# Meta queries transposed with the third block, output projections in held order with dealt-out splits, residual rows behind their group's weights

## The chip, the cores and the metric

The kernel runs on one core of one Trainium2 chip. The metric is the device time of one execution in microseconds (us); smaller is better. A core has five engines with a queue each, which run their instructions in order and wait for one another at semaphores: TensorE (PE: matrix products, with PEld for its weight loads), VectorE (DVE), ScalarE (ACT), GpSimd (POOL), and SyncE (SP), which here issues every transfer between the chip's memory and on-chip SBUF. Products land in PSUM, in banks of 512 float32 columns.

## The reference

Two layers of a hybrid decoder on 1024 tokens with 16 learned meta tokens ahead of them, so 1040 rows of 1024 numbers, float32.

```python
def hybrid_layer(x, ...):
    h = rms_norm(x, norm_g)
    z = h @ w_in                       # 1024 -> 6408 columns
    aq, ak, av, ag, mq, mk, mv, mi, mf, mo, mgate = split(z)
    q, k = rope(rms_norm(aq)), rope(rms_norm(ak))
    ya = sliding_window_sink_attention(q, k, av, sink) * silu(ag)     # 16 heads of 64, window 128
    mq, mk = silu(causal_depthwise_conv(mq, mk))
    hm = rms_norm(mlstm_chunkwise(mq, mk, mv, log_i, log_f))          # 4 heads, chunks of 64
    ym = hm * sigmoid(mo) * silu(mgate)
    return x + concatenate([ya, ym]) @ w_out                          # 2048 -> 1024 columns

def reference(x, meta, ...):
    h = concatenate([meta, x])
    for l in range(2):
        h = hybrid_layer(h, ...)
    return h[:, 16:]
```

Every query sees its window of 128 keys and all meta keys. In layer 0 the meta rows have queries of their own; in layer 1 they need none, since their outputs are dropped.

## The kernel before

The 1040 rows are nine tiles: tile 0 with the 16 meta rows, tiles 1 to 8 with 128 rows each (`TT`). Along the rows there are also three chunks of 272, 384 and 384 (`CH`); tiles 0 to 4 lie in the first two chunks, tiles 5 to 8 in the second and third. Every float32 product is made of a high part (a copy in the fp32r format, on ACT) and a low part (the remainder, a subtraction on DVE or POOL) of both operands, with three matmuls: high by high, high by low, low by high. So nearly every operand of PE comes with a *split*: a copy and a subtraction. Split activations stand in `H`, split weights in `RING`, which has eight slots of one weight tile. A weight arrives in one of two `raw` buffers.

A layer runs the key and value projection, then attention by pairs of heads (`j` = 0 to 7, the next projections woven between), then the mLSTM, then the output projection. PE's order in attention and mLSTM is written out by hand: `pin` keeps instructions in program order while `in_order[0]` is true (set at L1000, cleared at L1069). Elsewhere a scheduler that models the engines decides, before the kernel is built, in which order the instructions stand in each queue.

Attention of a pair goes by blocks of 128 queries (block 0 are the 16 meta queries, in layer 0 alone), in steps: `s1` the scores into bank S (L628), and the softmax; `s2` the transposes of the probabilities; `s3` and `s4` the products with the values into bank O (L692, L704), of which there is one, and the copies out of it. The next pair's meta queries are transposed by PE at L583 in step `s3` of block 5 into spare columns of that block's O bank, and `s4` of the block splits them with `q_put` (copies L561 and L562 on ACT, subtractions L563 and L564 on DVE). The next pair's scores of block 0 need the split.

The output projection multiplies 16 tiles of `k` (14 of them stored before in `spool` in memory, two in SBUF) with `w_out`. It first loads and splits all 16 times three chunks of y: load L1100, copy L1104, subtraction L1109 on DVE or, for every third `k`, on POOL. Then come four groups: tiles 0 to 4 (1 to 4 in layer 1) and tiles 5 to 8, each for the left and right half of 512 columns. In a group, 16 weights are loaded (L172), copied (L174, ACT) and subtracted (L175, every third on DVE, the others on POOL), and each is multiplied for all tiles of the group (L1135); in the last group the last eight weights are held and gone through tile by tile. The group's banks come from `pj`, `pss` and `po` in turn, two of each. At the end of a tile its residual rows are loaded (L1154), added on DVE (L1157) and stored (L1161, or the output at L1159). In layer 0 the square of the sum (L1162, ACT, written into the result's bank) gives the next norm: with the right half done, the left half is loaded back (L1165) and `norm_tile` scales (L285, DVE), transposes (L288, PE, eight per tile) and splits (L291 ACT, L292 DVE) into `H`.

Of the kernel before, what the change touches and what calls it, by code (L numbers as in the profile page):

```python
# [18 lines left out]
L = N_META + SEQ  # L19
# [43 lines left out]
def build(ctx, tc, I, O):  # L63
# [103 lines left out]

    def wout(l, k, c0, i):
# [3 lines left out]
        sy.dma_start(raw, I["w_out"][l][k * 128:(k + 1) * 128, c0:c0 + 512])  # L172
# [101 lines left out]
    def norm_tile(t, xh, ssq_ap, gbc):  # L274
# [5 lines left out]
        for g in range(2):  # L280
            if gbc is None:
                ve.tensor_scalar(xh[g][:p, :], xh[g][:p, :], v[:p, 1:2], None, ALU.mult)
            for i in range(2 if gbc is not None else 0):
                xs = xh[g][:p, 256 * i:256 * i + 256]
                ve.scalar_tensor_tensor(xs, xs, v[:p, 1:2], gbc[2 * g + i][:p, 0:256], ALU.mult, ALU.mult)  # L285
            ps = bank("pt")
            for k in range(4):
                pin(pe.transpose(ps[:, k * p:(k + 1) * p], xh[g][:p, k * 128:(k + 1) * 128], ident[:p, :p]))  # L288
            src = ps[:, 0:4 * p].rearrange("p (k t) -> p k t", k=4)
            hi = H[:, 4 * g:4 * g + 4, t0:t0 + p]  # L290
            sc.activation(hi, src, AF.Copy)  # L291
            ve.tensor_tensor(H[:, 8 + 4 * g:12 + 4 * g, t0:t0 + p], src, hi, op=ALU.subtract)  # L292
            if t == 0:
                for i in range(3):
                    ve.tensor_copy(HM[:, 4 * g:4 * g + 4, 16 * i:16 * i + 16],
                                   H[:, 4 * (g + i // 2 * 2):4 * (g + i // 2 * 2) + 4, 0:16])
# [15 lines left out]
    def first_norm(t, xt, G):  # L312
# [9 lines left out]
        norm_tile(t, xg, st[:p, 0:2], None)  # L322
# [29 lines left out]

    for l in range(DEPTH):
# [98 lines left out]
        def kv_tasks():  # L452
# [161 lines left out]
        def att_tasks(j, st):  # L614
# [67 lines left out]
            def s3(b):  # L682
# [3 lines left out]
                if b == 5 and j < 7 and first_q == 0:  # L686
# [407 lines left out]
        for i, k in enumerate(order):  # L1094
            ylo[k] = unit(F32R)
            for c, (t0, n, _) in enumerate(CH):
                a = s0 if c == 0 else t0
                if k < 14:
                    y = p512(F32, t0 + n - a) if (i + c) % 2 else t384(t0 + n - a)
                    sy.dma_start(y, spool[k, :, a:t0 + n])  # L1100
                else:
                    y = ym[k - 14][:, a:t0 + n]
                hi = H[:, k, a:t0 + n]
                sc.activation(hi, y, AF.Copy)  # L1104
                if a == 0:
                    sc.activation(ylo[k][:, L:L + 32], y[:, 0:32], AF.Copy)
                    gp.tensor_tensor(ylo[k][:, L + 32:L + 48], y[:, 0:16], ylo[k][:, L:L + 16], op=ALU.subtract)
                eng = gp if i % 3 == 2 else ve
                eng.tensor_tensor(ylo[k][:, a:t0 + n], y, hi, op=ALU.subtract)  # L1109
# [4 lines left out]
        pools = ["pj", "pss", "po"]  # L1114
        nb = 0
        for grp in (range(first_q, 5), range(5, 9)):
            for hf in range(2):
                c0 = 512 * hf
                pss_t = {}
                for t in grp:  # L1120
                    pss_t[t] = bank(pools[nb % 3])
                    nb += 1
                def product(i, k, t, w):
                    t0, p = TT[t]
                    ps = pss_t[t]
                    wh, wl = w
                    if t == 0:
                        st = ylo[k][:, L:L + 48]
                        terms = ((st, wh), (st, wl))
                        p = 48  # L1130
                    else:
                        hi, lo = H[:, k, t0:t0 + p], ylo[k][:, t0:t0 + p]
                        terms = ((hi, wh), (hi, wl), (lo, wh))
                    for n, (a, b) in enumerate(terms):
                        pin(pe.matmul(ps[:p, :], a, b, start=(i + n == 0), stop=(i == 15 and n == len(terms) - 1)))  # L1135

                cut = 16 - 8 if hf == 1 and grp[-1] == 8 else 16
                for i, k in enumerate(order[:cut]):
                    w = wout(l, k, c0, i)
                    for t in grp:  # L1140
                        product(i, k, t, w)
                tail = [(i, order[i], wout(l, order[i], c0, i)) for i in range(cut, 16)]
                for t in grp:
                    for i, k, w in tail:
                        product(i, k, t, w)
# [41 lines left out]
```

## Time and profile before

| | |
|---|---|
| runs, median of 3 | 1997.38 us (1996.06 to 1997.59) |
| the profiled execution, whole | 1995.97 us |
| its span, first to last instruction | 1994.2 us |
| PE busy | 1916.2 us, 96% |
| DVE, ACT, POOL busy | 1099.9, 1062.6, 929.9 us |
| mean granted TensorE clock | 0.99 |

PE is the engine to watch: what it does not work for is lost, while the others wait for some of the time anyway. In a row of the timeline, the square bracket holds the idle time of the engine just before that instruction and the instruction whose end released it. A row with x4 stands for four instructions that ran on end. A stretch's clock is a share of TensorE's full speed. Names such as `RING`, `raw` and `pj` are those of the code, and a line number is that of the instruction.

### The profile page before, as it was taken

What the parts mean: (1) busy time and instruction counts of PE and PEld (TensorE: products, weight loads), DVE (VectorE), ACT (ScalarE), POOL (GpSimd) and SP (SyncE); (2) the same over time, 40 slices, a digit from 0 to 9 for tenths busy, and PEclk for the clock granted to TensorE, in tenths of its full rate; (3) what the DMA queues carried; (4) which work ended last, traced back from release to release, by engine and by line L of the source; (5) the groups of instructions that cost most, each with busy time, mean ns of one, the idle gap of its engine ahead of it and who ended that gap; (6) DMA issues with size and microseconds to landing.
All of it is one profiled execution on the core that took longest, in us unless ns stands there. A gap on an engine that the chain in (4) does not pass through costs nothing. (4 is left out here: it accounts for less than half of the span.)

```text
span 1994.2 us, 36168 instructions
## 1 busy us (share of the span) xinstructions
PE 1916.2 (96%) x12823; PEld 1806.1 (91%) x12823; DVE 1099.9 (55%) x2969; ACT 1062.6 (53%) x3133; POOL 929.9 (47%) x1116
## 2 busy tenths in 40 slices
PE   6999899999999999989999999999999999999899
PEld 6899899999999999867879999999999999997787
DVE  8767767666445364541435677776573636347111
ACT  5567767655454544642324678777364545446221
POOL 7544544335555454553335345444365453646331
PEclk9999999999999999999999999999999999999999
DMA  5111111111212122453541111112122221217443
GB/s 160 43 33 42 42 44 37 35 53 45 57 47 69 36 59 58 146 170 115 162 144 49 48 36 51 45 36 58 38 58 62 39 76 38 61 47 232 145 141 106
DMA packets 149796, 147.71 MB, mean 74 GB/s; under 512 B 14952, under 2 KB 122768, under 8 KB 149616
## 3 DMA queue, kind: packets, MB, share of 16 engines
q1 hardware_dynamic: 149616, 145.41, 25.1%
q8 instruction: 101, 1.65, 0.4%
q14 instruction: 79, 0.65, 0.1%
HBM read 122.01 MB, written 23.29 MB: 73 GB/s over the span
## 5 line engine op out<-in xcount | busy, mean ns | idle before, releaser
L183 PE MATMUL pj<-H,RING 128*128 128x384 f32 (+2 forms) x3456 | 578.4, 323 | 0.3 <-ACT t L838 0.3
L183 PEld LDWEIGHTS pj<-H,RING 128*128 128x128 f32 x3456 | 546.1, 189 | 2.9 <-issue 0.7
L160 POOL TENSOR_TENSOR RING<-raw,RING 128x512 fp32r<-128x512 f32 (+1 forms) x196 | 260.6, 1337 | 137.8 <-ACT RING L159 125.4
L222 PE MATMUL pj<-RING,H 128*128 128x256 f32 (+1 forms) x1920 | 270.0, 287 | 1.9 <-DVE w1k L190 1.9
L222 PEld LDWEIGHTS pj<-RING,H 128*128 128x128 f32 x1920 | 244.0, 190 | 2.3 <-DVE w1k L190 2.2
L222 PE MATMUL pj<-H,RING 128*128 128x384 f32 (+2 forms) x1152 | 217.7, 327 | 3.0 <-DVE u L564 3.0
L175 POOL TENSOR_TENSOR RING<-raw,RING 128x512 fp32r<-128x512 f32 x88 | 115.0, 1311 | 196.8 <-ACT RING L174 192.4
L183 PE MATMUL pj<-RING,H 128*128 128x256 f32 x1536 | 200.8, 285 | 2.6 <-DVE H L292 1.5
L183 PEld LDWEIGHTS pj<-RING,H 128*128 128x128 f32 x1536 | 189.0, 189 | 4.0 <-DVE H L292 1.7
L174 ACT ACTIVATE RING<-raw 128x512 fp32r<-128x512 f32 x128 | 80.7, 632 | 202.2 <-DMA raw<-in_w_out_dram 134.1
L222 PEld LDWEIGHTS pj<-H,RING 128*128 128x128 f32 x1152 | 180.7, 191 | 3.8 <-PE T L668 1.3
L159 ACT ACTIVATE RING<-raw 128x512 fp32r<-128x512 f32 (+1 forms) x196 | 122.9, 629 | 73.3 <-DMA raw<-in_w_in_dram 48.2
L713 POOL TENSOR_TENSOR u<-u,w1k 128x128 f32<-128x128 f32 (+1 forms) x136 | 63.4, 466 | 176.8 <-DVE w1k L709 169.4
L175 DVE TENSOR_TENSOR RING<-raw,RING 128x512 fp32r<-128x512 f32 x40 | 31.5, 788 | 194.0 <-ACT RING L174 194.0
L679 POOL TENSOR_SCALAR_AFFINE_SELECT p<-p 128x512 fp32r<-128x512 f32 x112 | 72.2, 645 | 133.7 <-DVE p L675 131.1
L649 ACT ACTIVATE t<-S,mx 128x145 f32<-128x145 f32 (+1 forms) x272 | 100.3, 373 | 62.6 <-DVE mx L646 54.5
L882 POOL TENSOR_TENSOR p<-u,p 128x258 fp32r<-128x258 f32 x64 | 46.7, 730 | 169.2 <-ACT p L881 169.1
L1135 PE MATMUL pj<-RING,H 128*128 128x512 f32 x352 | 112.9, 400 | 7.1 <-DVE p L1157 5.8
L1135 PE MATMUL pss<-RING,H 128*128 128x512 f32 x352 | 113.5, 402 | 1.3 <-ACT H L1104 1.3
L824 DVE SCALAR_TENSOR_TENSOR t<-u,cw,t 128x384 f32<-128x384 f32 (+1 forms) x144 | 109.1, 757 | 2.6
L628 PE MATMUL S<-u 128*128 128x272 f32 (+2 forms) x544 | 87.5, 280 | 19.3 <-DVE u L563 16.3
L654 ACT ACTIVATE t<-t,mx 128x144 f32<-128x144 f32 (+1 forms) x272 | 97.6, 406 | 13.6 <-DVE mx L651 13.1
(342 smaller groups left out, 3834.0 us busy)
## 6 DMA issues: line engine op xcount, KB each, us to landing
raw<-in_w_out_dram SPq DMA_DIRECT2D x128, 256.0 KB, 2.8
raw<-in_w_in_dram SPq DMA_DIRECT2D x100, 256.0 KB, 2.8
raw<-in_w_in_dram SPq DMA_DIRECT2D x192, 128.0 KB, 2.3
spool<-u SPq DMA_DIRECT2D x56, 192.0 KB, 1.9
p<-x SPq DMA_DIRECT2D x24, 256.0 KB, 4.4
t<-spool SPq DMA_DIRECT2D x28, 192.0 KB, 3.5
p<-spool SPq DMA_DIRECT2D x28, 192.0 KB, 3.6
u<-em SPq DMA_DIRECT2D x8, 576.0 KB, 6.9
```

What stands on the lines that cost most here:

```text
L159: sc.activation(hi, raw[:, :, 0:o], AF.Copy)
L160: eng.tensor_tensor(lo, raw[:, :, 0:o], hi, op=ALU.subtract)
L174: sc.activation(hi, raw, AF.Copy)
L175: (ve if i % 3 == 2 else gp).tensor_tensor(lo, raw, hi, op=ALU.subtract)
L183: pin(pe.matmul(out, a, b, start=(i == 0), stop=(i == n - 1)))
L222: pin(pe.matmul(out(), x, y, start=(k + i == 0), stop=(k == n - 1 and i == 2)))
L628: pin(pe.matmul(S[:p, h, o + 2 - 2 * h:o + 2 - 2 * h + kn], lq, Ks[i][:, k0:k0 + kn], start=(i == 0), stop=(i == 1)))
L649: sc.activation(P[:p, 145 * h:145 * h + 145], S[:p, h, 1 + 127 * h:146 + 127 * h], AF.Exp, bias=mx[:p, 0, h:h + 1], accum_out=mx[:p, 1, h: ...
L654: sc.activation(Pn, Pn, AF.Copy, scale=mx[:p, 2, h:h + 1])
L679: gp.affine_select(OW, HL, [[0, 4], [1, 128]], ALU.is_ge, 0.0, base=0, channel_multiplier=-1)
L824: ve.scalar_tensor_tensor(z, RAW[:, t0 + i:t0 + i + n], wcol(i), z, ALU.mult, ALU.add)
L1135: pin(pe.matmul(ps[:p, :], a, b, start=(i + n == 0), stop=(i == 15 and n == len(terms) - 1)))
```

## The change

Three things, in the words of the diff's own parts. First, the meta queries are transposed in step `s3` of block 3 rather than 5, and split in `s4` of the same block.

```diff
-                if b == 5 and j < 7 and first_q == 0:
+                if b == 3 and j < 7 and first_q == 0:
                     st["QM"] = O[:, 256:272]
                     q_meta_turn(j + 1, st["QM"])
```

PE, attention of the first pair in layer 0, before (L583 is the transpose, S_1077 x4 of 16x16 the scores of the meta queries, L222 the woven projection):

```order
L222 MATMUL pj<-H,RING 128x384 x6
L583 MATMUL O<-cst,w1k 128x16
L692 MATMUL O<-p_1473,u 128x256 x2
L704 MATMUL O<-ptm_107,VM 128x128 x2
L704 MATMUL O<-p_1478,u 128x256 x2
L206 MATMUL pj<-RING,HM 48x256 x16
L628 MATMUL S_1077<-u 16x16 x4
```

and now (L594 is the transpose; the scores stand 25 rows behind it, after the same 16 matmuls of 48x256, L208):

```order
L594 MATMUL O<-cst,w1k 128x16
L703 MATMUL O<-p_1333,u 128x256 x2
L224 MATMUL pj<-H,RING 128x384 x6
L715 MATMUL O<-ptm_107,VM 128x128 x2
L715 MATMUL O<-p_1338,u 128x256 x2
...
L703 MATMUL O<-p_1479,u 128x256 x2
L715 MATMUL O<-ptm_107,VM 128x128 x2
L715 MATMUL O<-p_1484,u 128x256 x2
L208 MATMUL pj<-RING,HM 48x256 x16
L639 MATMUL S_1077<-u 16x16 x4
```

The transpose moved two blocks ahead; the scores did not move.

Second, the output projection. The y splits become a function of one `k` and one chunk, and are dealt to the groups: chunks 0 and 1 to the first, each pair ahead of its weight, chunk 2 to the second. Banks go round two by two. The last three weights of a group (six in the fourth) are held and gone through tile by tile. PE's order is the program's from the second group on. Of the weights' subtractions, the first nine of a group are POOL's, and of the rest every second is DVE's. The square goes to a bank of the tag `pt`. Residual rows are issued behind the group's last weight:

```diff
-        (ve if i % 3 == 2 else gp).tensor_tensor(lo, raw, hi, op=ALU.subtract)
+        (ve if i > 8 and i % 2 else gp).tensor_tensor(lo, raw, hi, op=ALU.subtract)
...
-        pools = ["pj", "pss", "po"]
+        pools = ["pj", "pj", "pss", "pss", "po", "po"]
...
+            with tc.issue_after(w_load[0]):
+                sy.dma_start(xr[:p, :], src)
...
+            in_order[0] = g > 0
...
+            cut = 10 if g == 3 else 13
+            chunks = ((0, 1), (2,), (), ())[g]
+            for i in range(cut):
+                for c in chunks:
+                    y_split(i, c)
+                w = wout(l, order[i], c0, i)
                 for t in grp:
+                    product(pss_t[t], i, t, w)
+                if g == 2 and not last:
+                    if i > 2:
+                        turn()
+                    if i % 2 and i < 10:
+                        norm_again(i // 2)
...
+            for t in grp:
+                for i, w in tail:
+                    product(pss_t[t], i, t, w)
+                    if g == 3 and i == 12:
+                        turn(3)
+                if g == 3:
+                    turn(2)
+                result(pss_t[t], t, hf)
+        in_order[0] = False
+        carry[:] = turns
```

SP's queue at the end of layer 0's first group, before (L172 loads a weight, L1100 a chunk of y, L1154 residual rows, L1161 stores a sum):

```order
L172 DMA raw<-in_w_out_dram 128x512
L1100 DMA p_11131<-spool 128x384
L1154 DMA p_11437<-in_meta_dram 16x512
L172 DMA raw<-in_w_out_dram 128x512
L1154 DMA p_11443<-in_x_dram 128x512
L1154 DMA p_11448<-in_x_dram 128x512
L1154 DMA p_11453<-in_x_dram 128x512
L172 DMA raw<-in_w_out_dram 128x512 x11
L1161 DMA x_96<-p_11443 128x512
```

and now (L174, L1115, L1159, L1170 are the same four):

```order
L1115 DMA t<-spool 128x384 x3
L174 DMA raw<-in_w_out_dram 128x512 x2
L1115 DMA t<-spool 128x384 x3
L174 DMA raw<-in_w_out_dram 128x512 x2
L1159 DMA p_11341<-in_meta_dram 16x512
L1159 DMA p_11357<-in_x_dram 128x512
L1159 DMA p_11372<-in_x_dram 128x512
L1159 DMA p_11387<-in_x_dram 128x512
L174 DMA raw<-in_w_out_dram 128x512 x7
L1170 DMA x_96<-p_11341 16x512
```

The residual rows stand behind all sixteen weights of their group now, where before weights of the group came after them.

DVE's queue between the first and the second group of layer 1, before (L1109 is a y subtraction, L175 a weight's, L1157 the addition of the residual rows, which frees a bank):

```order
L1109 TENSOR_TENSOR u<-p_22731,H 128x256
L1109 TENSOR_TENSOR u<-p_22739,H 128x384
L175 TENSOR_TENSOR RING<-raw,RING 128x512 x2
L1157 TENSOR_TENSOR p_23003<-pj,p_23003 128x512
L1157 TENSOR_TENSOR p_23007<-pss,p_23007 128x512
L1157 TENSOR_TENSOR p_23011<-po,p_23011 128x512
L1157 TENSOR_TENSOR p_23015<-pj,p_23015 128x512
```

and now (L1124, L177, L1162):

```order
L177 TENSOR_TENSOR RING<-raw,RING 128x512
L1162 TENSOR_TENSOR p_22952<-pj,p_22952 128x512
L1162 TENSOR_TENSOR p_22965<-pj,p_22965 128x512
L1162 TENSOR_TENSOR p_22978<-pss,p_22978 128x512
L1124 TENSOR_TENSOR u<-p_23019,H 128x384
L1162 TENSOR_TENSOR p_22991<-pss,p_22991 128x512
```

Before, two subtractions of weights of the second group stood ahead of the adds; now none does, and y subtractions of chunk 2 stand among and behind them.

Third, the norm at the end of layer 0. `norm_tile` is cut into `norm_pre` (the scale factor and the scaling) and `norm_half` (four transposes and the split of one half). Tiles 0 to 4, whose sums are complete after the second group, are loaded back and normed in the third (`norm_again` after weights 1, 3, 5, 7 and 9, one half after each of the weights 3 to 12). Tiles 5 to 8 are normed in the fourth, a half at a time within the tail of a later tile, and the last three halves, in `carry`, between the tiles of layer 1's key and value projection:

```diff
                 ps = projN(wg, t, 256)
+                if l > 0 and t != 1 and carry:
+                    carry.pop(0)()
                 ve.tensor_copy(KR[:p, t, :], ps[:p, 0:128])
```

The number of matmuls and transposes is the same as before. For tiles 5 to 8 the left half is loaded back as two transfers of 256 columns; for tiles 0 to 4 both halves are loaded back.

## Rows read from the trace of the kernel before

**Rows 1.** The page: busy us, share of the span, instructions

```profile
PE 1916.2 (96%) x12823; PEld 1806.1 (91%) x12823; DVE 1099.9 (55%) x2969; ACT 1062.6 (53%) x3133; POOL 929.9 (47%) x1116
```

**Rows 2.** Waits: engine, line, waited for: us in total, times, longest

```profile
PE S L628 <- DVE u L563: 16.3, 8, 5.9
...
PE pj L1135 <- POOL RING L175: 2.3, 1, 2.3
...
PE po L1135 <- ACT RING L174: 1.8, 1, 1.8
...
PE po L1135 <- POOL RING L175: 1.3, 2, 0.7
```

**Rows 3.** Timeline of PE: start, us, operation, count, [idle before <-releaser]

```profile
103.70 0.40 PE L692 MATMUL O<-p,u 128*128 128x256 f32 x2
...
108.45 0.49 PE L692 MATMUL O<-p,u 128*128 128x256 f32 x2
...
119.50 0.23 PE L583 MATMUL O<-cst,w1k 16*128 16x16 f32 x1
...
123.42 0.49 PE L628 MATMUL S<-u 128*16 128x16 f32 x4 [0.93 <-DVE u L563]
...
239.42 0.23 PE L583 MATMUL O<-cst,w1k 16*128 16x16 f32 x1
...
248.27 0.50 PE L628 MATMUL S<-u 128*16 128x16 f32 x4 [5.90 <-DVE u L563]
...
1109.38 0.52 PE L628 MATMUL S<-u 128*128 128x272 f32 x2 [0.95 <-DVE u L563]
```

**Rows 4.** Timeline of ACT at the longest wait

```profile
246.74 0.63 ACT L159 ACTIVATE RING<-raw 128x512 fp32r<-128x512 f32 x1 [0.58 <-DMA raw<-in_w_in_dram]
```

**Rows 5.** Stretches: us, busy of PE PEld DVE ACT POOL, clock, DMA, GB/s

```profile
244.80:251.60 6.80, 3.25 (x17) 3.11 (x18) 3.24 (x12) 3.42 (x12) 6.63 (x7) 0.50 0.37 106
330.20:333.60 3.40, 3.40 (x17) 3.33 (x17) 2.12 (x5) 0.87 (x4) 3.40 (x3) 0.51 0.22 65
890.00:896.80 6.80, 5.11 (x11) 2.95 (x12) 3.85 (x6) 4.48 (x11) 2.54 (x2) 0.50 0.55 186
1047.00:1050.40 3.40, 3.33 (x16) 3.33 (x17) 3.10 (x7) 2.26 (x6) 1.40 (x2) 0.51 0.33 84
1855.90:1862.70 6.80, 5.14 (x12) 4.12 (x13) 3.08 (x5) 1.66 (x4) 2.55 (x2) 0.50 0.63 204
100.00:400.00 300.00, 282.51 (x2160) 274.61 (x2159) 211.65 (x639) 213.53 (x724) 129.28 (x180) 0.98 0.14 39
1100.00:1400.00 300.00, 291.33 (x2235) 286.84 (x2235) 214.06 (x616) 215.05 (x702) 130.78 (x171) 0.99 0.16 45
```

**Rows 6.** Timeline of SP's queue and ACT, layer 0's first output group

```profile
863.96 1.41 SPq L1154 DMA_DIRECT2D p<-in_x_dram  x3
...
866.01 0.63 ACT L174 ACTIVATE RING<-raw 128x512 fp32r<-128x512 f32 x1 [3.88 <-DMA raw<-in_w_out_dram]
```

**Rows 7.** Timeline of DVE and PE, last norm of layer 0

```profile
1042.66 3.75 DVE L285 SCALAR_TENSOR_TENSOR p<-p,nv,w1k 128x256 f32<-128x256 f32 x4 [0.73 <-POOL nv L279]
...
1047.07 1.97 PE L288 MATMUL pt<-cst,p 128*128 128x128 f32 x8 [2.00 <-DVE H L292]
```

**Rows 8.** Timeline of DVE and PE, layer 1's output projection

```profile
1836.43 1.50 DVE L175 TENSOR_TENSOR RING<-raw,RING 128x512 fp32r<-128x512 f32 x1
...
1856.21 0.69 DVE L175 TENSOR_TENSOR RING<-raw,RING 128x512 fp32r<-128x512 f32 x1 [8.16 <-ACT RING L174]
...
1857.56 1.22 PE L1135 MATMUL pj<-RING,H 128*128 128x512 f32 x2 [5.85 <-DVE p L1157]
```

**Rows 9.** By line: ns min/median/max, first and last start; us to landing

```profile
L175 POOL TENSOR_TENSOR RING<-raw,RING x88: 1257/1292/1734, 797.4 to 1969.1; 128x512 fp32r<-128x512 f32 x88
...
DMA to landing us min/median/max: 2.7/3.3/6.4
```

**Rows 10.** The chain that ended last: start, us, engine, tile, line, count

```profile
1870.14 1.39 PE pss L1135 x6
```

More of the change, by code (lines that the diff above doesn't have):

```diff
@@ L166, in wgroup @@
         return [(ps[k // 2][:, 0, k % 2], ps[k // 2][:, 1, k % 2]) for k in range(8)]
+    w_load = [None]
     def wout(l, k, c0, i):
@@ L321, in first_norm @@
             xg.append(y)
-        norm_tile(t, xg, st[:p, 0:2], None)
+        norm_pre(t, xg, st[:p, 0:2], None)
+        for g in range(2):
+            norm_half(t, g, xg[g:g + 1])
     snk = cp.tile([128, 2, HEADS], F32, name="snk")
@@ new lines, in build, with product @@
+        pools = ["pj", "pj", "pss", "pss", "po", "po"]
+        nb = [0]
+        turns = []
+        def product(ps, i, t, w):
+            k = order[i]
+            t0, p = TT[t]
+            wh, wl = w
+            if t == 0:
+                st = ylo[k][:, L:L + 48]
+                terms = ((st, wh), (st, wl))
+                p = 48
+            else:
+                hi, lo = H[:, k, t0:t0 + p], ylo[k][:, t0:t0 + p]
+                terms = ((hi, wh), (hi, wl), (lo, wh))
+            for n, (a, b) in enumerate(terms):
+                pin(pe.matmul(ps[:p, :], a, b, start=(i + n == 0), stop=(i == 15 and n == len(terms) - 1)))
@@ new lines, in result @@
+        def result(ps, t, hf):
+            t0, p = TT[t]
+            c0 = 512 * hf
+            xr = p512(F32)
+            if l > 0:
+                src = x1[t0:t0 + p, c0:c0 + 512]
+            elif t == 0:
+                src = I["meta"][:, c0:c0 + 512]
+            else:
+                src = I["x"][t0 - 16:t0 + 112, c0:c0 + 512]
+            with tc.issue_after(w_load[0]):
+                sy.dma_start(xr[:p, :], src)
+            if t == 0:
+                ve.tensor_tensor(xr[:16, :], ps[32:48, :], xr[:16, :], op=ALU.add)
+            ve.tensor_tensor(xr[:p, :], ps[:p, :], xr[:p, :], op=ALU.add)
+            if last:
+                sy.dma_start(O["out"][t0 - 16:t0 + 112, c0:c0 + 512], xr[:p, :])
+                return
+            if hf == 1 and t > 4:
+                x0 = [t384(256) for _ in range(2)]
+                for i, x in enumerate(x0):
+                    sy.dma_start(x[:p, :], x1[t0:t0 + p, 256 * i:256 * i + 256])
+            sy.dma_start(x1[t0:t0 + p, c0:c0 + 512], xr[:p, :])
+            sc.activation(bank("pt")[:p, :], xr[:p, :], AF.Square, accum_out=ssq[:p, t, hf:hf + 1])
+            if hf == 1 and t > 4:
+                norm_later(t, x0 + [xr[:, 0:256], xr[:, 256:512]])
@@ new lines, in norm_later, with norm_again, turn @@
+        def norm_later(t, xq):
+            norm_pre(t, xq, ssq[:TT[t][1], t, :], gbc)
+            turns.extend(lambda g=g: norm_half(t, g, xq[2 * g:2 * g + 2]) for g in range(2))
+        def norm_again(t):
+            t0, p = TT[t]
+            x = [p512(F32) for _ in range(2)]
+            for i in range(2):
+                sy.dma_start(x[i][:p, :], x1[t0:t0 + p, 512 * i:512 * i + 512])
+            norm_later(t, [y[:, o:o + 256] for y in x for o in (0, 256)])
+        def turn(least=1):
+            if len(turns) >= least:
+                turns.pop(0)()
```

133 lines of the change are left out of this document (49 added, 84 removed).

## The prediction

> **What bounds the kernel now.** I read the busy shares first: TensorE (PE) works for 96% of the span of 1994.2 us, the other engines for about half of it [rows 1]. 1994.2 − 1916.2 = 78.0 us of PE idle is thus all that a change which leaves the matmuls alone can win, with what TensorE loses while its clock is at the lower of its two levels. None of the edits takes matmuls out, so I looked for the idle stretches and their releasers, engine by engine: first the list of waits, then the timeline of PE at each wait, then the granted clock by stretches. Four places belong to lines that the diff touches.
>
> First, the attention of layer 0. The scores of the meta queries wait for a subtraction on VectorE (DVE) that makes their split: 16.3 us in eight waits [rows 2]. One of them, 0.95 us, is in layer 1 [rows 3], which has no meta queries, so 16.3 − 0.95 = 15.35 us in seven waits. The pattern is the first one: the transpose runs at 119.50, the scores at 123.42, that is 3.9 us later, 0.93 us of it idle. The worst has its transpose at 239.42 and its scores 8.85 us later, after 5.90 us of idle [rows 3]: there ScalarE's (ACT) queue held a weight split that waited for its own transfer [rows 4] ahead of the copy that frees the query.
>
> Second, the output projection of layer 0: 2.3, 1.8 and twice some 0.65 us (1.3 together) on weights that come late, 5.4 us [rows 2]. Just ahead of the first of them three residual rows are issued between the weights, and ACT then waits 3.88 us for a weight [rows 6]. Third, the last norm of layer 0: PE waits 2.00 us for the subtraction of a half that stands behind a scaling of 3.75 us on DVE [rows 7]. Fourth, the output projection of layer 1: 5.85 us at the start of the second group, for the adds that free the banks; DVE reached the add only when a weight subtraction ahead of it in its queue had run, after DVE had waited 8.16 us for that weight [rows 8].
>
> After most of these idles the granted clock is 0.50 for 3.4 or 6.8 us and 1.0 outside: the 1.2 GHz level instead of 2.4 [rows 5]. PE's work of such a stretch takes twice as long, so half of its busy time is lost: 3.25/2 = 1.6 us behind the wait at 248, 3.40/2 = 1.7 behind one at 329, 5.11/2 = 2.55 in layer 0's projection, 3.33/2 = 1.65 at the norm, 5.14/2 = 2.55 in layer 1's.
>
> **The change, part by part.**
>
> Meta queries two blocks earlier. It is the same number of instructions. The transpose (one instruction, 0.23 us) moves ahead of the third block's second matmuls, and the copies and subtractions on ACT and DVE follow it there, while the scores stay where they are, behind two more blocks of PE's work. Blocks follow one another by 108.45 − 103.70 = 4.75 us [rows 3], so the split has 9.5 us more, against a longest wait of 5.90. The wait goes: 15.35 + 1.6 + 1.7 = 18.7 us. It is not given for nothing: query columns lie in the O bank, of which there is one, and the next block's matmuls into it wait until the split has read them. That was so at the old place as well, with the same 3.9 us from transpose to split, under 4.75. If that cover is gone, the wait sits at the new place (a rival). What is late next are the waits that layer 1 has: its 300 us of attention hold 300 − 291.33 = 8.7 us of idle, layer 0's 300 − 282.51 = 17.5 [rows 5], of which 15.35 are ours, hence 2.1 of others. If layer 0 takes on layer 1's idle, 6.6 us come back; if not, none. The work on the other engines is alike, but layer 0's waits now cover up what layer 1's would show, so I take the middle, 3.3 us.
>
> Output projections of layer 0. The third chunk's 16 loads and splits leave the first group for the second, the residual loads go behind the group's last weight, and the nine first subtractions go to GpSimd (POOL). Groups take 16 weights; 12 matmuls a weight at 1.39/6 = 0.232 us [rows 10] are 2.8 us for a four-tile group, and 14 are 3.2 us with five tiles. A subtraction on POOL is 1.29 us [rows 9], so POOL keeps the pace. The four late weights come from loads queued behind other loads and from splits queued behind others, and both go: 5.4 + 2.55 = 7.9 us. Lower bound of this gain: if only the residual rows mattered, the first stall of 2.3; upper: 7.9, which I take, since weights now stand ahead of all that delayed them.
>
> The square goes to a bank of its own and six banks are dealt out in turn rather than three, so the second half of a group starts on free banks. It has no price of its own.
>
> Norm of layer 0 into the third group and the next layer's projection. The same transposes (eight a tile, nine tiles) are issued in halves between matmuls; PE pays for them as before. Nine reloads become ten of the same size and eight of half of it, on SP's queue behind weights. The last norm's wait is gone: 2.00 + 1.65 = 3.65 us. New waits: in the fourth group, the first half of tile 5 must be scaled within one tile's tail, 6 weights x 3 matmuls x 0.232 = 4.2 us, while the four scalings alone have taken up to 3.75 [rows 7]; and the turns in the next layer's projection stand on PE ahead of its tiles. I charge 0 to 2 us, and take 1.
>
> Layer 1. In the changed order the four adds stand ahead of any of the next group's subtractions on DVE, since its nine first weights are POOL's. The wait of 5.85 us and its lower clock go: 5.85 + 2.55 = 8.4 us. What is late next is the weight itself: the first group now holds three weights to its end and needs the last of them some 4 us earlier. The loads ahead of them on SP are fewer by 14 chunks, at 1.41/3 = 0.47 us of issue each [rows 6], so I take 0 and leave up to 3 us.
>
> Here a rule bears against the change. The rows show a weight's subtraction on DVE at 1.50 us in a stretch in which POOL subtracts too, where the same instruction takes 0.69 at another time [rows 8], and POOL's at up to 1.73 where 1.29 is the median [rows 9]. The Trainium skill, page "SBUF — State Buffer", section "Who interferes with whom", says that a DVE instruction with two SBUF inputs and a GpSimd instruction that reads SBUF exclude each other, one waiting until the other has ended; the rows agree. What the mechanism would cost here is rival E.
>
> **Sum.** 18.7 − 3.3 + 7.9 + 3.65 − 1 + 8.4 = 34.3 us. It is made against the profiled execution, 1995.97 us (span 1994.2 and 1.8 around it): 1961.6. The median of the runs, 1997.38, is 1.4 above that execution, so the forecast is 1963 us, 1.7% less.
>
> **The rivals.**
>
> A. The meta wait moves with the transpose: the O bank is held, and the next block's matmuls wait instead of the scores. For it: 3.9 us to the split against 4.75 between blocks leaves under 1 us, and the worst took 8.85. Against it: the bank was held in the same way at the old place, and no such wait is in the list for that line. It costs the 18.7 − 3.3 = 15.4 us: 1978.
>
> B. Supply of weights binds in the output projections: two raw buffers, held from the load's issue to the end of the subtraction, so that taking DVE's 0.69 out of the first nine puts weights late whatever the queue order. For it: ACT's wait of 3.88 [rows 6]. Against it: a load of that size lands in 2.7 to 3.3 us [rows 9], ACT's copy takes 0.63 [rows 6] and POOL 1.29, 4.6 to 5.2 together, over two buffers 2.3 to 2.6 a weight, and PE needs 2.8. Only attention and norm remain, 15.4 + 2.65 = 18.05 us: 1979.
>
> C. Slower. The reloads of the third group come late. There PE's order is fixed, ten half-tile turns stand between the products, and a reload that is late stops PE at each; the next weights stand behind it on SP. A row of that size lands in 3.3 us, at worst 6.4 [rows 9], and is scaled in up to 3.75 [rows 7]; from the turn that frees its buffers it has two steps of PE, 5.6 us. 3.3 + 3.75 − 5.6 = 1.5 us a turn are possible. From 34.3/10 = 3.4 us a turn on the whole gain is eaten; with the worst landing it is 6.4 + 3.75 − 5.6 = 4.6, and the ten cost 46 us: 1963 + 46 = 2009. Against it: the sums of squares of these tiles are complete a group earlier, and SP runs weights ahead of PE.
>
> D. It does not do what it says: new waits in the fixed order eat what goes, within 4 us (0.2%) of 1997, about what a measurement of this kernel can tell from no change.
>
> E. DVE and POOL hold each other up. Three more of each group's weights are POOL's, 3 x 1.29 = 3.9 us in which DVE's splits wait. In the first group of each layer PE needs those splits at once, so the two first groups lose 2 x 3.9 = 7.7 us: 1971. For it: the stretched subtractions above. Against it: POOL's 12 x 1.29 and DVE's 4 x 0.69 make 18.2 us even one after the other, in a group of 44 to 52, and a third of the splits leaves the first group.
>
> **How the numbers follow.** Forecast 0.67; A 0.10; B 0.09; C 0.04; D 0.04; E 0.06. The forecast's own range: low, where nothing comes back and no new wait appears (−4.3) and a further 1.7 us of a lower clock goes with the waits, 1957; I put 1955. High, 6.6 coming back, 2 of new waits, 3 in layer 1 and 2.3 instead of 7.9 in layer 0, +3.3 + 1 + 3 + 5.6: 1976. E lies inside; A and B end at 1979, which I take as the end. C and D lie outside. Faster 0.92, same 0.04, slower 0.04.
>
> **What would show it.** In the trace of after: the list of waits has no wait of the scores for the split above 1 us in total, and layer 0's 300 us of attention show PE at about 294 to 297 (right), or a wait of the second matmuls for VectorE's subtraction near 15 us (A). The projections show no idle above 1 us and no 0.50 clock at the starts of groups (right), or waits for the subtraction on GpSimd (B). In the third group of layer 0, a transpose that waits for a scaling or for a reload is C. The adds of layer 1 run within 1 us of their product's end (right). The forecast falls, in the good direction, if other idle of the 78 us goes as well; in the bad one, if the 0.50 clock appears in new places, as a stretch costs 1.7 to 2.6 us even where the idle before it is short.

## The result

The changed kernel takes 1969.84 us (median of 4 executions, 1967.16 to 1971.40) where the one before takes 1997.49 in the same comparison: a ratio of 0.9861 with a 95% interval of 0.9844 to 0.9878. That is 27.65 us less, where 34.3 were forecast; the time lies in the range, above the forecast of 1963. Its profiled execution took 1971.03 us, 24.9 below that of the kernel before.

The page of the changed kernel, first part (busy us, share of the span, instructions), against [rows 1]:

```profile
span 1969.3 us, 36180 instructions
...
PE 1906.4 (97%) x12823; PEld 1795.8 (91%) x12823; DVE 1099.3 (56%) x2961; ACT 1062.8 (54%) x3133; POOL 940.8 (48%) x1124
```

PE's idle time is now 1969.3 − 1906.4 = 62.9 us, 15.1 less. Its busy time is 9.8 us less for the same 12823 instructions, and it runs less of the time at the lower clock. By stretches of 2 us, the granted clock of before falls below 0.9 in nine places; after, two are left ahead of the last instructions, at 57 to 61 and at 409 to 413 us.

The waits of PE in the attention of layer 0, from the first scores to the last products with the values (engine, line, waited for: us, times, longest), against the wait of the scores in [rows 2]:

```profile
PE O L703 <- DVE w1k L720: 4.1, 5, 1.7
PE T L676 <- DVE ptm L687: 3.7, 2, 2.8
PE pj L224 <- DVE u L612: 2.7, 2, 1.5
PE O L703 <- DVE u L575: 2.6, 4, 1.1
PE pj L224 <- DVE u L575: 2.1, 2, 1.2
```

The scores' wait for the split, 15.4 us in seven times, is gone altogether. In its place stand waits for VectorE that the trace before had little of: of these lines that trace lists in the same stretch

```profile
PE S L628 <- DVE u L563: 15.4, 7, 5.9
PE T L665 <- DVE ptm L676: 2.8, 1, 2.8
...
PE pj L222 <- DVE u L564: 0.9, 2, 0.5
PE O L692 <- DVE w1k L709: 0.5, 1, 0.5
```

Idle time against idle time, by stretches (us, then busy time of PE, PEld, DVE, ACT, POOL, clock, DMA share, GB/s): layer 0's attention; layer 0's output projection up to the first scores of layer 1; layer 1's output projection; of the changed kernel also layer 1's attention. Before:

```profile
85.70:427.70 342.00, 320.48 (x2422) 311.65 (x2421) 238.32 (x717) 239.92 (x805) 147.29 (x202) 0.98 0.15 41
825.70:1094.60 268.90, 258.94 (x1345) 213.51 (x1345) 114.70 (x221) 105.42 (x237) 115.03 (x114) 0.98 0.45 141
1796.80:1992.00 195.20, 185.59 (x790) 149.46 (x789) 56.80 (x85) 59.20 (x118) 73.57 (x59) 0.97 0.50 158
```

after:

```profile
86.00:422.00 336.00, 318.02 (x2422) 308.81 (x2421) 239.51 (x718) 239.72 (x806) 147.04 (x202) 0.99 0.15 42
818.80:1079.40 260.60, 256.03 (x1346) 210.81 (x1345) 118.09 (x219) 105.03 (x237) 120.44 (x117) 1.00 0.48 149
1780.20:1968.00 187.80, 182.62 (x790) 146.26 (x789) 53.87 (x83) 59.24 (x118) 74.44 (x62) 1.00 0.53 165
1079.40:1391.00 311.60, 300.62 (x2310) 295.67 (x2309) 222.81 (x637) 220.72 (x718) 136.42 (x176) 1.00 0.16 45
```

The attention went from 342.0 to 336.0 us, of which 342.0 − 320.5 = 21.5 and 336.0 − 318.0 = 18.0 idle. The projection and norm of layer 0 went from 268.9 to 260.6 us, its idle time from 10.0 to 4.6; layer 1's projection from 195.2 to 187.8, its idle time from 9.6 to 5.2. So 6.0 + 8.3 + 7.4 = 21.7 of the 24.9 us lie in the three places; the other 3.2 are spread over work that did not change.

Where the attention's gain went shows at a single place. Before, at the end of the third pair (start, us, engine, operation, [idle before <-releaser]):

```profile
200.59 2.03 PE L206 MATMUL pj<-RING,HM 128*48 128x256 f32 x16
203.96 0.49 PE L628 MATMUL S<-u 128*16 128x16 f32 x4 [1.34 <-DVE u L563]
204.31 0.96 PE L222 MATMUL pj<-RING,H 128*128 128x256 f32 x6
```

after, the same instructions:

```profile
200.59 2.03 PE L208 MATMUL pj<-RING,HM 128*48 128x256 f32 x16
202.46 0.25 PE L639 MATMUL S<-u 128*16 128x16 f32 x4
203.89 0.98 PE L224 MATMUL pj<-RING,H 128*128 128x256 f32 x6 [1.18 <-DVE u L612]
```

The scores start 1.5 us earlier, at 202.46 against 203.96. But the projection's matmuls right behind them gained 0.42 us (203.89 against 204.31), since they need a bank of `pj` that VectorE's gating multiplication (L601 before, L612 after) has to read first, and that ran where it had run before:

```profile
203.15 0.55 DVE L601 SCALAR_TENSOR_TENSOR u<-t,pj 128x384 f32<-128x384 f32 x1 [0.22 <-ACT t L600]
```

```profile
203.28 0.56 DVE L612 SCALAR_TENSOR_TENSOR u<-t,pj 128x384 f32<-128x384 f32 x1 [0.22 <-ACT t L611]
```

The wait of the scores had covered this second wait.

### The profile page after: what moved, and what is told of

Read it like the earlier page. It is cut to its first block, busy times and chain, and to the rows that moved or that the text cites. A ratio compares the mean times of both kernels' runs of the same rounds, so it can differ in the third digit from the quotient of the medians.

```text
span 1969.3 us, 36180 instructions
## 1 busy us (share of the span) xinstructions
PE 1906.4 (97%) x12823; PEld 1795.8 (91%) x12823; DVE 1099.3 (56%) x2961; ACT 1062.8 (54%) x3133; POOL 940.8 (48%) x1124
## 3 DMA queue, kind: packets, MB, share of 16 engines
q8 instruction: 101, 1.65, 0.4%
## 5 line engine op out<-in xcount | busy, mean ns | idle before, releaser
L177 POOL TENSOR_TENSOR RING<-raw,RING 128x512 fp32r<-128x512 f32 x96 | 125.8, 1316 | 177.6 <-ACT RING L176 165.2
L1145 PE MATMUL pss<-RING,H 128*128 128x512 f32 x384 | 120.5, 395 | 0.3 <-ACT H L1119 0.3
L720 DVE TENSOR_TENSOR w1k<-O,w1k 64x128 f32<-64x128 f32 (+1 forms) x272 | 74.6, 274 | 38.7 <-ACT w1k L718 36.0
L853 DVE SCALAR_TENSOR_TENSOR t<-t,pj 128x384 f32<-128x384 f32 (+2 forms) x48 | 24.5, 510 | 126.5 <-ACT t L852 126.5
```

The lines of the kernel that those rows point to most:

```text
L177: (ve if i > 8 and i % 2 else gp).tensor_tensor(lo, raw, hi, op=ALU.subtract)
L720: ve.tensor_tensor(y[64 * h:64 * h + 64, :p], O[0:64, p * h:p * h + p], up[0:64, p * h:p * h + p], op=ALU.add)
```

## The experiments

All are built on one of the two kernels. A ratio compares a kernel with runs of the kernel before that were made beside it on the same chip. Times of different comparisons are less alike: the kernel before has medians from 1995.5 to 1997.5 us in them. The changed kernel stands at 0.9861 (0.9844 to 0.9878).

**Part 1 alone, and the rest alone.** Two kernels tell what each half of the diff is worth.

```diff
 kernel before, e1_meta_only
-                if b == 5 and j < 7 and first_q == 0:
+                if b == 3 and j < 7 and first_q == 0:
 changed kernel, e2_rest_only
-                if b == 3 and j < 7 and first_q == 0:
+                if b == 5 and j < 7 and first_q == 0:
```

> The kernel before with the meta queries transposed in block 3 and nothing else. The forecast's term for this edit was 15.4 us, which would give about 1982 us. The landmarks of the traces (last matmul of layer 0's attention 427.4 us before, 421.7 after) say 6 us, which would give about 1991. In the trace the scores' wait for the split (15.4 us) should be gone either way; if 1991 is right, some 10 us of other, smaller waits of PE must stand in layer 0's attention that were not there before.

> The changed kernel with the meta queries back in block 5: the output projections and the norm alone. By the forecast's terms 8.4 + 7.9 + 3.65 - 1 = 19 us less than before, about 1978 us; by the landmarks of the traces some 19 to 21 us, 1976 to 1978. If the parts add, this and the run before it together make the whole difference of 27.6 us.

Measured: the meta queries alone 1987.97 us, ratio 0.9961 (0.9948 to 0.9974), 8 us less; the rest alone 1973.55 us, ratio 0.9887 (0.9873 to 0.9902), 22.5 us less. Together 30.5, about the whole. So the term of the attention was 8 us and not 15.4, between the two figures expected, and the rest gave 22.5 where the sum had 19. In the traces the attention takes 337.1 us and 344.7 us, and the seven waits of the scores are absent in the one and 15.2 us in the other. The late weights of layer 0 and the wait of 5.8 us for the adds of layer 1 are still there with part 1 alone, and gone in the rest alone.

One trace is one execution, and stretches of the same code differ between them. With the meta queries at block 5 the attention of layer 0 takes 342.0 and 344.7 us; with them at block 3 and no other edit in the attention, nine traces have 334.5 to 337.1 us, 16.7 to 18.0 of it idle. The lowest idle time of these:

```profile
83.40:419.60 336.20, 319.47 (x2422) 310.59 (x2420) 238.93 (x718) 239.42 (x806) 146.34 (x202) 0.99 0.15 42
```

So by the traces the gain of the attention lies between 5 and 10 us, with the 8 us of the run in the middle; the 6.0 of one pair is no better than that.

**Is it the O bank?** The transpose goes to spare columns of a bank of scores.

```diff
-                    st["QM"] = O[:, 256:272]
+                    st["QM"] = SS[0][:, 1, 480:496]
```

> The changed kernel with the meta queries transposed into spare columns of a bank of scores, not into the one O bank. Theory 1 (the gain of the attention went to waits that any head start of PE would meet, on the copies and subtractions of ACT and DVE): no difference, 1968 to 1971 us; the 2.6 us in which the second matmuls wait for the split move elsewhere. Theory 2 (rival A in part: the split holds the O bank, which the next block's matmuls need): 2.6 us of that wait and the 3.6 us by which their wait for the copies out of O grew go, about 1964 us.

Measured: 1969.72 us, ratio 0.9868 (0.9851 to 0.9884), no difference. PE's waits in its attention:

```profile
PE T L676 <- DVE ptm L687: 4.1, 2, 3.2
PE S L594 <- ACT t L660: 3.8, 4, 1.4
PE pj L224 <- DVE u L612: 3.5, 3, 1.2
PE O L703 <- DVE w1k L720: 3.4, 4, 1.7
```

The wait of the second matmuls for the split (L703 on L575) is gone, and 3.8 us of the transpose for the exponentials that read the scores' bank came for it. So this run doesn't free the split of a bank, it changes the bank, and the time did not change. In its trace the attention is 5.2 us longer than the changed kernel's, 341.2 us, and other stretches of the same code are shorter. What speaks against rival A is thus the size of the wait for the split in the O bank, 2.6 us of 15.4; what a bank of its own would give is not shown.

**What is left of the meta queries.** No transpose and no split for pairs 1 to 7:

```diff
-                if b == 3 and j < 7 and first_q == 0:
+                if False:
...
-                    lq = U[:, 1024 + 16 * h:1040 + 16 * h] if b == 0 else ...
+                    lq = VM[:, 0, 0, 0:16] if b == 0 and j > 0 else U[:, 1024 + 16 * h:1040 + 16 * h] if b == 0 else ...
```

> The changed kernel without the meta queries of pairs 1 to 7 in layer 0: no transpose, no split, and their scores take constant columns in place of the queries, so that part of the result is left out. It shows what all that is left of the meta queries costs. Theory 1: PE's idle in layer 0's attention stays at 14 us or more of 18, and the time falls by under 3 us, 1967 to 1970. Theory 2: the waits that came new, some 10 us, are the split's own, and the time falls to about 1960 to 1963.

Measured: 1959.79 us, ratio 0.9823 (0.9808 to 0.9838). The two halves of the expectation came apart: the time is that of theory 2, PE's idle time that of theory 1. PE's waits in the attention, and the stretch:

```profile
PE T L676 <- DVE ptm L687: 4.4, 2, 3.4
PE pj L224 <- DVE u L612: 3.9, 3, 1.5
PE O L703 <- DVE w1k L720: 3.0, 3, 1.7
PE pj L224 <- DVE u L575: 2.1, 2, 1.2
```

```profile
84.40:415.90 331.50, 315.27 (x2415) 308.14 (x2413) 236.56 (x704) 236.72 (x792) 146.68 (x202) 0.99 0.15 42
```

331.5 − 315.3 = 16.2 us of idle time are left without any split, against 18.0 with it at block 3 and 21.5 with it at block 5. All of the waits for L612, L687 and L720 are here, in a kernel in which nothing can wait for a meta query. So by this trace 21.5 − 16.2 = 5.3 us of the 15.4 were to be had as idle time; the other 10 stood in front of waits for other work of VectorE. That the run is faster than the changed kernel, by 10 us of the medians and 0.0038 of the ratios (some 7.6 us), is not explained by this: the attention is 336.0 − 331.5 = 4.5 us shorter, of which 1.8 is idle and 2.7 busy time of PE (seven transposes of 0.23 us are 1.6 of it), and the rest lies in stretches that are the same code in both, such as the 86.0 us ahead of the attention, which took 84.4 us here: the changed kernel's lower clock at 57 to 61 us is not in this trace. What makes the executions differ there stays open.

**Is it ScalarE's queue?** Some of the weights' copies during attention and mLSTM go to GpSimd.

```diff
-        sc.activation(hi, raw[:, :, 0:o], AF.Copy)
+        if in_order[0] and kt % 4:
+            gp.tensor_copy(hi, raw[:, :, 0:o])
+        else:
+            sc.activation(hi, raw[:, :, 0:o], AF.Copy)
```

> The changed kernel with half of the weight copies of attention and mLSTM (0.63 us each on ScalarE) on GpSimd instead. Theory 1 says that PE's small waits in layer 0's attention stand for the queues of ScalarE and VectorE; the waits' releasers are VectorE's instructions, which wait for ScalarE's copies. If ScalarE's queue is what holds them, PE's idle there falls from 18 to under 14 us and the time to 1962 to 1967 us. If VectorE's own work is it, no difference, 1968 to 1971; if GpSimd's longer work holds VectorE up or makes weights late, slower, 1972 or more.

The edit reached fewer weights than the expectation says, 40 of 196: 15 of the 34 in each layer's attention and none in the mLSTM. `in_order[0]` is false there; it is cleared when the attention ends, and not behind the mLSTM as the description of the kernel before has it. Measured: 1964.91 us, ratio 0.9834 (0.9819 to 0.9849). The stretches (layer 0's attention, layer 1's) and the copy itself, by line:

```profile
83.50:418.30 334.80, 318.85 (x2423) 309.41 (x2421) 240.93 (x718) 231.91 (x791) 156.85 (x217) 0.99 0.14 42
1072.40:1384.00 311.60, 302.92 (x2317) 298.05 (x2316) 225.28 (x638) 213.22 (x704) 145.17 (x191) 0.99 0.16 45
```

```profile
L160 POOL CAST RING<-raw x40: 608/613/1078, 33.4 to 1329.7; 128x512 fp32r<-128x512 f32 x36, 128x528 fp32r<-128x528 f32 x4
```

ScalarE has 239.7 − 231.9 = 7.8 us less to do in layer 0's attention and PE's idle time is 334.8 − 318.9 = 15.9 us, 2.1 less than 18.0; in layer 1's it is 311.6 − 302.9 = 8.7, where the changed kernel has 311.6 − 300.6 = 11.0. The time is what ScalarE's queue was expected to give, the idle time half of it. But neither attention is shorter than in traces without this edit: layer 0's lies among the 334.5 to 337.1 us above, with 0.8 us less idle than the lowest of them, and layer 1's is as long as the changed kernel's. ScalarE's queue may be a part of these waits; it isn't shown, and the gain in time lies mostly outside the two stretches. With the kernel that holds no weights to a group's end, below, it is the fastest here that does the whole computation; the intervals of both overlap that of the changed kernel a little, and the two edits together were not tried.

**The edits of the output projections, one undone at a time.**

```diff
 e5_split_rule
-        (ve if i > 8 and i % 2 else gp).tensor_tensor(lo, raw, hi, op=ALU.subtract)
+        (ve if i % 3 == 2 else gp).tensor_tensor(lo, raw, hi, op=ALU.subtract)
 e6_rows_not_held
-            with tc.issue_after(w_load[0]):
-                sy.dma_start(xr[:p, :], src)
+            sy.dma_start(xr[:p, :], src)
 e8_three_banks
-        pools = ["pj", "pj", "pss", "pss", "po", "po"]
+        pools = ["pj", "pss", "po"]
...
-            sc.activation(bank("pt")[:p, :], xr[:p, :], AF.Square, accum_out=ssq[:p, t, hf:hf + 1])
+            sc.activation(ps[:p, :], xr[:p, :], AF.Square, accum_out=ssq[:p, t, hf:hf + 1])
 e10_all_interleaved
-            cut = 10 if g == 3 else 13
+            cut = 10 if g == 3 else 16
 e11_y_in_first_group
-            chunks = ((0, 1), (2,), (), ())[g]
+            chunks = ((0, 1, 2), (), (), ())[g]
 e12_free_order
-            in_order[0] = g > 0
+            in_order[0] = False
```

> The changed kernel with the weights' subtractions shared out as before (every third on VectorE from the first on). If it was the subtractions ahead of the adds in VectorE's queue that made layer 1's wait of 5.85 us and its lower clock, some of the 8.4 us come back, 1974 to 1978 us. If the banks in turn by two and the held weights did that, no difference, 1968 to 1971. If VectorE and GpSimd hold each other up (rival E), this one is up to 8 us faster, 1962.

> The changed kernel with the residual rows not held behind the group's last weight. If their place in the queue made layer 0's late weights, about 2.3 to 5 us and a lower clock of 2.5 come back, 1972 to 1977 us. If the dealt-out chunks of y did that, no difference, 1968 to 1971.

> The changed kernel with the groups' banks dealt out as before (pj, pss, po in turn) and the square written into the result's bank. If the banks' order costs nothing by itself, as the forecast said, 1968 to 1971 us; if a second half must then wait for the square of the first, 2 to 6 us more.

> The changed kernel with no weights held to the end in the first three groups (all sixteen gone through for all tiles; only the last group keeps its six). Undoing the share-out of subtractions and the queue place of the residual rows cost nothing, the banks 7 us. If it is the tile by tile end of a group that frees banks in time and so took away layer 1's wait of 5.85 us with its lower clock, that wait or one like it comes back at the three inner ends of groups in each layer: 5 to 20 us more, 1975 to 1990. If the turn of banks alone does it, no difference, 1968 to 1971.

> The changed kernel with all three chunks of y loaded and split in the first group. If the third chunk's place among the weights was what made layer 0's weights late (5.4 us of waits and 2.55 of clock), about 5 to 8 us come back in layer 0, and some in layer 1, 1975 to 1980 us. If not, no difference, 1968 to 1971.

> The changed kernel with PE's order in the output projections left to the scheduler, all else as changed. If the held order is what makes the gain of the projections, 5 to 15 us come back, 1975 to 1985 us; if the other edits make it, no difference, 1968 to 1971.

| undone | us | ratio (95%) |
|---|---|---|
| share-out of subtractions | 1968.19 | 0.9868 (0.9849 to 0.9887) |
| residual rows held | 1971.61 | 0.9882 (0.9860 to 0.9903) |
| banks two by two | 1977.11 | 0.9909 (0.9885 to 0.9933) |
| weights held to a group's end | 1965.29 | 0.9834 (0.9818 to 0.9851) |
| chunks of y dealt out | 1973.21 | 0.9877 (0.9859 to 0.9895) |
| held order of PE | 1971.09 | 0.9869 (0.9855 to 0.9884) |

Only the banks give something back that stands clear; the intervals of the rows and of the chunks of y leave a few us open. The run undoes two edits at once, the order of the banks and the place of the square. The row of it, at the start of layer 0's second group, with VectorE's add that used the same bank and ScalarE's queue behind it:

```profile
871.70 0.69 DVE L1162 TENSOR_TENSOR p<-pj,p 128x512 f32<-128x512 f32 x1 [1.39 <-PE pj L1145]
...
880.89 0.52 ACT L1119 ACTIVATE H<-p 128x384 fp32r<-128x384 f32 x1 [6.26 <-DMA p<-spool]
...
881.84 0.58 ACT L1171 ACTIVATE pj<-p 128x512 f32<-128x512 f32 x1
...
882.60 1.22 PE L1145 MATMUL pj<-RING,H 128*128 128x512 f32 x2 [6.35 <-ACT pj L1171]
```

PE waits 6.35 us for a square that ScalarE writes into the bank which the next half needs. The add had read that bank by 872.4 us, before PE came to need it at 876.25; the square came 9.5 us later, behind the copy of a chunk of y that waited for its transfer. So by this trace it is the square's place that costs, in a queue where y is now split between the groups. What the order of the banks is worth by itself was not run.

Holding the weights to a group's end gains nothing that shows: without it the kernel is about 4.5 us faster by the medians, with intervals that overlap a little, and without the waits for weights in layer 1's second group. The longest of those is, in the changed kernel:

```profile
1844.31 0.50 PE L1145 MATMUL po<-RING,H 128*128 128x512 f32 x1 [0.85 <-POOL RING L177]
```

Kernels with the same projections have less of them: the rest alone, above, holds the weights as well and has none.

None of the six brings back layer 1's wait of 5.85 us for the adds [rows 8] nor layer 0's late weights of 5.4 us [rows 2]. The largest of the kind are 3.2 us in layer 1 with the rows not held, where layer 1's projection also takes 190.5 us from its first product, 4.4 more than in any other trace that holds them, and 3.5 us over both layers with all of y in the first group. So none of the six is needed by itself to remove either wait. Either more than one of them is enough, or it is an edit that no run undid: y split weight by weight within a group, and no longer ahead of all the groups. Pairs were not tried. The cause of the projections' gain is settled only as far as this: the waits and the lower clock behind them go with these edits together, and no single one of the six is what removes them.

**The norm done at once, as before, with all else changed.**

```diff
-            if hf == 1 and t > 4:
-                x0 = [t384(256) for _ in range(2)]
...
-                norm_later(t, x0 + [xr[:, 0:256], xr[:, 256:512]])
+            if hf == 1:
+                x0 = p512(F32)
+                sy.dma_start(x0[:p, :], x1[t0:t0 + p, 0:512])
+                norm_pre(t, [y[:, o:o + 256] for y in (x0, xr) for o in (0, 256)], ssq[:p, t, :], gbc)
+                was, in_order[0] = in_order[0], False
+                for g2 in range(2):
+                    norm_half(t, g2, [(x0, xr)[g2][:, 0:256], (x0, xr)[g2][:, 256:512]])
+                in_order[0] = was
...
-                    if i % 2 and i < 10:
-                        norm_again(i // 2)
```

> The changed kernel with the norm of layer 0 done at once behind each right half, as before, with its transposes free in PE's order; everything else as changed. By the forecast this part was worth 3.65 - 1 = 2.65 us, so about 1972.5 us. If the traces' landmarks are right that layer 0's projection and norm gained some 10 us together and the queues' part of it is the 5.4 us of waits and 2.55 of clock, it is again 2 to 4 us, 1972 to 1974.

Measured: 2011.78 us, ratio 1.0087 (1.0065 to 1.0108), slower than the kernel before and 42 us slower than the changed one. PE's waits from layer 0's projection on, and one of the places:

```profile
PE pt L294 <- issue: 19.9, 7, 3.2
PE pt L294 <- DVE p L286: 6.1, 3, 3.7
```

```profile
930.48 1.92 PE L294 MATMUL pt<-cst,p 128*128 128x128 f32 x8 [3.12 <-issue]
```

Each tile's eight transposes now stand between the products of a group, and PE waits up to 3.7 us ahead of them, 26 us in all. For most of it the profile names no releaser ("issue"), but in the wait shown the tile's own add starts on VectorE at 927.39, the square follows on ScalarE, and the scaling starts at 929.89. Behind the waits the transposes run at the lower clock (1.92 us for eight, where eight took 1.97 at the lower clock before [rows 7]). That is akin to rival C: a turn that comes too early for its scaling, in an order that holds everything behind it, though here no reload of the third group is late. In the changed kernel the turns wait 2.5 us altogether:

```profile
PE pt L294 <- DVE H L298: 1.1, 2, 0.7
PE pt L294 <- DVE t L286: 0.8, 1, 0.8
PE pt L294 <- ACT pt L1171: 0.6, 2, 0.3
```

## Why the prediction was right, and what was off in it

- **The reading of before** held: the four places named were the places where the time went, the scores' wait is gone to the last tenth, and the stretches at half clock in the projections went with the waits.
- **Attention: 15.4 us forecast, 8 by the run with this part alone, 6.0 by the two traces.** The lead came out about as worked out: the scores now stand 12.0 to 13.7 us behind the transpose, where they stood 3.9 to 8.9 us behind it, waits included. The step that failed is the give-back, "the middle, 3.3 us", between none and 6.6. Its upper end was taken from layer 1, whose idle time in attention was held to be what layer 0 could fall to. The run without any meta split has 16.2 us of idle, 10 more than the trace before shows beside the scores' waits. So the give-back was 18.0 − 6.1 = 12 us of waits: the time of 15.4 us was listed under one releaser, but two thirds of it stood over other waits that end at nearly the same moment. The prediction's own sign says the same: PE was to be busy for 294 to 297 of the 300 us from 100 to 400, and it is for 286.0, after 282.5. Of the clock's 3.3 us, both stretches are gone in the trace of the changed kernel, and the one at 416 us, which was not the meta queries', is still there at 409. But with part 1 alone the clock stands at 0.57 from 244 to 248 us, behind waits of 0.88 and 1.69 us; the changed kernel has the same two waits there and a clock of 1.00. So that 1.6 us is not sure to go.
- **Layer 0's projection and norm: 7.9 + 3.65 − 1 = 10.55 us forecast, 8.3 measured** in the two traces. No late weight is left. The charge of 1 us for new waits was 2.5, the turns' waits above; four other kernels with the same projections have 0.6 to 1.2.
- **"It has no price of its own", of the square and the banks,** was wrong for the changed kernel: undone together they cost 7 us, and the trace puts it on the square.
- **The norm's part** was priced at 2.65 us. Against the kernel before that can't be told apart from the rest, but undone under the held order it is 42 us. That is the price of the old norm in the new order, which the sum had no term for; the held order itself gains nothing that shows (1971.09 us without it), and both undone together were not run.
- **Layer 1: 8.4 us forecast, 7.4 measured** in the projection's stretch. The waits for weights are 1.4 us, within the 0 to 3 left for the weights that are held. The reason given, the share-out of subtractions that takes them from in front of the adds, isn't needed: with the old share-out the wait doesn't come back. And the sign, adds within 1 us of their product's end, failed for the fourth add of the first group: its product ended at 1829.2, and it ran 13.7 us later, since a subtraction of y stood ahead of it in VectorE's queue. PE lost nothing by it, since the second group works in the banks of `po` and `pj`. The adds of the third and the fourth tile:

```profile
1827.11 0.69 DVE L1162 TENSOR_TENSOR p<-pss,p 128x512 f32<-128x512 f32 x1 [1.34 <-PE pss L1145]
1842.41 0.56 DVE L1124 TENSOR_TENSOR u<-p,H 128x384 fp32r<-128x384 f32 x1 [14.61 <-ACT H L1119]
1842.89 0.68 DVE L1162 TENSOR_TENSOR p<-pss,p 128x512 f32<-128x512 f32 x1
```

- **Rivals.** A: 2.6 us of it are in the trace of the changed kernel (L703 waits for L575), a sixth of its price. B: 1.2 us. C did not happen here. E did not show: by it the kernel with the old share-out should be up to 8 us faster, and it is 1.65 us faster by the medians and not at all by the ratios, with intervals that overlap nearly whole, so nothing of E's price shows in the time. The prediction counted three more subtractions a group for GpSimd; that holds for the first nine weights, but over the group it is one more (96 against 88 in eight groups). The Trainium skill, page "SBUF — State Buffer", section "Who interferes with whom", has a VectorE instruction with two inputs in SBUF and a GpSimd instruction that reads SBUF exclude each other. The stretched subtractions in the trace of before agree with it [rows 8].
- **The whole:** 34.3 forecast, 27.65 measured. The missing 6.7 are about the attention's give-back, 15.4 − 8 = 7.4. The projections' sum of 19 is not told apart as finely: 22.5 by the run with these parts alone, 15.7 by the traces of before and after. That the whole came within 7 us of the forecast, although the attention gave half of its term, is in part luck: by the run the projections gave 3.5 us more than their sum, for which the prediction has no reason.

## What to carry to other kernels

A wait in the list is worth what stands behind it when it is gone, not its length: ask of each wait when the next instruction's own operands are ready, and follow the same engines for a few microseconds past it; here, with ACT and DVE at 70% in the stretch, two thirds of the wait was cover for their next results. The bound on what comes back is better taken from a kernel that leaves the waited-for work out than from a neighbouring layer that looks alike. And a set of edits can be worth much together while undoing most of them singly costs nothing that shows, so an undo of one doesn't price it. One trace of each kernel is not enough for terms of a few us: stretches of the same code differ by as much.

## What the runs showed of the hardware that was not expected

GpSimd copies a weight tile of 128x512 from float32 to fp32r in 0.61 us, as fast as ScalarE (0.63 us) and in half the time of its own subtraction of that size (1.29 us, [rows 9]).

And the length of the waits does not tell whether the clock falls behind them. In the kernel before, PE comes to the output projection of each layer with the same two waits, 0.6 us of matmuls between them and back-to-back matmuls ahead of them. Layer 0, layer 1, and the stretches behind the second wait (columns as above):

```profile
828.26 0.63 PE L869 MATMUL po<-p,w1k 128*128 128x258 f32 x3 [1.08 <-DVE w1k L933]
830.14 0.73 PE L1135 MATMUL pss<-RING,H 128*128 128x512 f32 x2 [1.25 <-ACT H L1104]
```

```profile
1799.36 0.62 PE L869 MATMUL po<-p,w1k 128*128 128x258 f32 x3 [1.07 <-DVE w1k L933]
1801.25 1.22 PE L1135 MATMUL pj<-RING,H 128*128 128x512 f32 x2 [1.27 <-ACT H L1104]
```

```profile
830.10:833.50 3.40, 3.36 (x16) 2.45 (x16) 3.34 (x10) 3.40 (x13) 2.85 (x5) 1.00 0.99 319
1801.30:1804.70 3.40, 3.40 (x10) 2.83 (x11) 2.23 (x6) 2.93 (x10) 2.06 (x3) 0.50 0.94 313
```

The clock stays at 1.00 in layer 0 and stands at 0.50 in layer 1, and the pair of matmuls behind the wait takes 0.73 us in the one and 1.22 in the other. A single wait of 2.25 us for a late weight, at 867 us, leaves it at 1.00. So a term for the lower clock behind a short wait is a chance, not a certainty; what decides it is not shown here.
